# Split-operand attention scores, a query norm folded into the exponential, and weights split earlier in a one-core decoder layer

## The chip, the cores and the metric

The kernel runs on one core of a Trainium2 chip. The metric is device time of one execution in microseconds (us). The kernel before took 1689.93 us, the median of three runs (1689.31 to 1690.85).

## The reference

One layer of a hybrid decoder is computed for 1024 prompt tokens and 32 sample tokens (8 requests of 4), 1056 columns in all, with D = 1024: RMS norm, retention and gated linear recurrence with a common input projection, output projection and residual; then cross-attention into 256 memory tokens, and a SwiGLU feed-forward. The change touches the cross-attention (4 heads of 256 channels):

```python
m = _rmsnorm(mem, g_mem); k = (m @ w_xk); v = (m @ w_xv)            # memory keys and values, also outputs
q = (_rmsnorm(x, g_xa) @ w_xq).reshape(b, t, XA_HEADS, XA_HD)
s = einsum('bthd,bmhd->bhtm', q, mk) * (XA_HD ** -0.5)
p = softmax(s, axis=-1); o = einsum('bhtm,bmhd->bthd', p, mv)
x = x + o.reshape(b, t, -1) @ w_xo
```

Prompt tokens attend to the memory keys made here; each sample request has its own keys and values, read from a cache.

## The kernel before, in words

Activations lie with channels on the 128 partitions and tokens along the free dimension: eight tiles of 128 x 1056. Most products are made of split operands: a float32 number is written as a high part `h` (rounded to float32r by a ScalarE copy) and a low part `l` (the difference, by VectorE or GpSimd), and `mms` (line 226) does three single passes per product: hh, hl and lh. Some small products, the prompt scores among them, are plain float32 matmuls; the trace shows two records for each of these.

An `Item` is one block of 128 output channels: its weights come from DRAM in two halves of 256 KB (`wraw`, four buffers, by SyncE's queue), are split into `wh` (ScalarE) and `wl` (GpSimd, VectorE or one half each, by the item's `l_eng`), and are multiplied with all columns in groups of 384, 384 and 288. `run` goes through the items in order; the weights of the next item are split after the first piece of the present item (`w_split`), and those of a later one are loaded after its second group. The schedule is written by hand: each engine executes its instructions in the order in which the program issues them. Side work is written as generators; `tick()`, called after each piece of an item, advances every generator to its next `yield`. So "two yields" means two pieces later. An item in `c_items` has six pieces; the query items have twelve; an item with steps (`k_outer`) goes over k outermost, with a tick after each k.

The stages that matter, in order of time:

- `k_items` and `v_items` (about 520 to 580 us): memory keys and values, 256 columns. The key tile `k32` is kept in float32, and stored to the output `mk_o` from there.
- `c_items` (about 580 to 673 us): output projection with residual (line 993). ScalarE squares the sum (`sg`), GpSimd adds it to `acc` (line 340). The weights' low halves are made by GpSimd alone. Beside it runs `split_ahead`: it splits weights that are needed much later (17 blocks: ten halves of `w_xo`, seven of sums of `w_gate`) and stores both halves to DRAM (`pre_d`): load `praw`, `pwh` on ScalarE, `pwl` on GpSimd, two yields, two stores, then `PACE` = 3 more yields; two buffers each for `pwh` and `pwl`. After four items, the sample keys (`keyT`) and values (`vb`) are loaded too.
- `xq_items` (about 673 to 833 us): query projection; its first item is a `k_outer` whose steps split the normed-to-be input (`xh` on ScalarE, `xl` on VectorE, line 320). `rstd_bcast` (line 344) sums `acc` over channels on TensorE, takes the power -1/2 on GpSimd (line 327), broadcasts the factors of all columns to 128 partitions on TensorE (line 331), and copies them to `rbc`; the evacuation of every query item multiplies by it (line 1021).
- `attend(h)` runs as side work during the later query items and the first items after them: `stage_a` (scores, line 1194, row maximum, exponential), `stage_n` (division), `stage_b` (transposes of the probabilities and their split), `stage_c` (product with the split values). Each step of its list is two ticks apart. `sample_attend` does the same for the sample tokens, with the float32 queries.
- `ea_items`, `eb_items` (from about 833 us): product with `w_xo`; the second part reads the halves from `pre_d`.

Of the kernel before, what the change touches and what calls it, by code (L numbers as in the profile page):

```python
# [18 lines left out]
P = 128  # L19
# [28 lines left out]
LEAD = 3  # L48
LEADW = 3
KEYS = 4  # L50
PACE = 3
QUADS = ((0, 1), (0, 0), (1, 1), (1, 0))
DVE_L = 672
W1 = 4
# [41 lines left out]
def build(tc, ctx, a, outs):  # L96
# [4 lines left out]
    def newpool(name, bufs=1, stack=ctx, **kw):  # L101
        return stack.enter_context(tc.tile_pool(name=name, bufs=bufs, **kw))
# [17 lines left out]
    def sm():  # L120
        return psum("sm", 3)
# [7 lines left out]
    def tmp(nm):  # L129
        return gz.tile([P, GW], F32, name=nm, tag=nm)  # L130
# [4 lines left out]
    def btile(i, shape=None, dt=F32):  # L135
        return bp.tile(shape or [P, T], dt, name=f"b{i}", tag=f"b{i}")
# [20 lines left out]
    def side(gen):  # L157
        sides.append(gen)
        return gen
# [112 lines left out]
    def run(items):  # L272

        for it in items:
            i = done[0]
            assert wq[i] is it
            if it.start:
                it.start()
            w = splits.pop(i)
            if it.steps:  # L280
                k_outer(it, w)
            else:
                for n_, g in enumerate(it.order or range(len(it.cols))):
                    group(it, w, g, n_ == 0)
                    if n_ == 1:
                        w_raw()
            if it.steps or len(it.cols) < 2:
                w_raw()
            done[0] += 1
            if it.end:  # L290
                it.end()
# [630 lines left out]
    def mem_split():  # L922

        hh, ll = [[xtile(w_, k) for w_ in "hl"] for k in (3, 2)]
        kvs["memh"], kvs["meml"] = ([x[:, :4 * NMEM].rearrange("p (k t) -> p k t", k=4) for x in xx] for xx in (hh, ll))
        pt = sm()
        for i in range(2):
            bcast_cols(pt[:, i * P:(i + 1) * P], kvs["mr"][:, i:i + 1], P)
        kvs["rbm"] = tp.tile([P, T], F32, name="rbc", tag="rbc", bufs=1)
        dve.tensor_copy(kvs["rbm"][:, :NMEM], pt[:, :NMEM])  # L930
        kvs["k32"] = [btile(i, [P, 4, NMEM]) for i in range(2)]
        kvs["vh"] = [btile(2, [P, D], F32R), btile(3, [P, D], F32R)]

    def mem_split_k(k):
# [2 lines left out]
        act.activation(h_, src, AF.Copy, scale=gain("g_mem", k))  # L937
        dve.scalar_tensor_tensor(l_, src, gain("g_mem", k), h_.bitcast(F32), op0=ALU.mult, op1=ALU.subtract)

    def k32(m):  # L940
        return kvs["k32"][m // 4][:, m % 4]

    def kv_proj_item(wname, m, is_k, l_eng):
        def ev(pt, g):
            if is_k:
                t32 = k32(m)
            else:
                t32 = tmp("sg")[:, :NMEM]
            dve.tensor_tensor(t32, pt, kvs["rbm"][:, :NMEM], op=ALU.mult)

            def rest():
                yield
                if is_k:
                    yield
                    sp.dma_start(mk_o[m], t32)
                    return
                tt = sm()[:, :NMEM]
                for i in range(2):
                    pe.transpose(tt[:, i * P:(i + 1) * P], t32[:, i * P:(i + 1) * P], ident)
                st = tmp("z")[:, :NMEM]  # L960
                act.activation(st, tt, AF.Copy)
                ms = slice(m * P, (m + 1) * P)
                for i in range(2):
                    act.activation(kvs["vh"][i][:, ms], tt[:, i * P:(i + 1) * P], AF.Copy)
                    dve.tensor_tensor(kvs["vl"][i][:, ms], tt[:, i * P:(i + 1) * P], kvs["vh"][i][:, ms].bitcast(F32), op=ALU.subtract)
                yield
                sp.dma_start(mv_o[0, 0].rearrange("(i p) h d -> p i (h d)", p=P)[:, :, ms], st.rearrange("p (i e) -> p i e", i=2))

            side(rest())

        def start():
            if m == 0 and is_k:
                mem_split()
            if m == 0 and not is_k:
                kvs["vl"] = [btile(4, [P, D], F32R), btile(5, [P, D], F32R)]

        def mem_xs():
            return ([kvs[w_][k // 4][:, k % 4] for k in range(KT)] for w_ in ("memh", "meml"))

        it = Item(a[wname][m], KT, mem_xs, ev, cols=(slice(0, NMEM),), l_eng=l_eng, start=start)  # L980
        if is_k and m == 0:
            it.stepwise(range(KT), [lambda k=k: mem_split_k(k) for k in range(KT)])
        return it
# [27 lines left out]
                for b, order in enumerate(EB) for m in order]  # L1011
    for it in eb_items:
        it.l_eng, it.wide = "dve", True
    q32 = {}

    def xq_item(m):
        def start():
            q32[m] = act_tile(m)

        def ev(pt, g):  # L1020
            dve.tensor_tensor(q32[m][:, GS[g]], pt, rb["t"][:, GS[g]], op=ALU.mult)

        return Item(a["w_xq"][m], KT, xs, ev, start=start)

# [75 lines left out]
    def split_ahead():  # L1100
        jobs = [a["w_xo"][m][:, ks.start + (KH if m < XA else 0):ks.stop + (KH if m < XA else 0)]
                for m in range(KT) for ks in halves(KH if m < XA else KT)]

        def load(src):
            t = kv.tile([P, KH, P], F32, name="praw", tag="praw", bufs=4)
            sp.dma_start(t, src)
            return t

        def split(n, src):
            h_, l_ = (kv.tile([P, KH, P], F32R, name=nm, tag=nm, bufs=2) for nm in ("pwh", "pwl"))  # L1110
            split2(h_, l_, src, pool)
            yield
            yield
            for i, t in enumerate((h_, l_)):
                sp.dma_start(pre_d[n, i], t.bitcast(F32))
            for _ in range(PACE):
                yield

        raw = [load(j) for j in jobs[:2]]
        yield  # L1120
        yield
        for n in range(len(jobs)):
            yield from split(n, raw.pop(0))
            if n + 2 < len(jobs):
                raw.append(load(jobs[n + 2]))
        a21, a11, a22, a12 = [load(a["w_gate"][c][:, r * KH:(r + 1) * KH]) for r, c in QUADS]
        yield
        yield
        sm_ = kv.tile([P, KH, P], F32, name="psm", bufs=1)
        n0 = len(jobs)  # L1130
        at = {no: n0 + PRODUCTS.index(no) for no in PRODUCTS}
        pool.tensor_tensor(sm_, a21, a22, op=ALU.add)
        yield from split(at[5], sm_)
        pool.tensor_tensor(a21, a11, a21, op=ALU.subtract)
        yield from split(at[7], a21)
        yield from split(at[1], a11)
        pool.tensor_tensor(sm_, sm_, a11, op=ALU.subtract)
        yield from split(at[6], sm_)
        yield from split(at[4], a22)
        yield from split(at[2], a12)  # L1140
        pool.tensor_tensor(sm_, a12, sm_, op=ALU.subtract)
        yield from split(at[3], sm_)
# [17 lines left out]
        split_cols((new_x["h"][k], new_x["l"][k]), src, slice(0, T), scale)  # L1160

    xq_items[0].stepwise(ORD, [lambda k=k: split_next(k, st_c["x"][k], gain("g_xa", k)) for k in ORD], c_items[-1])
    side(split_ahead())
    run(c_items[:KEYS])
    load_values(0, 0)
    side(sample_keys())
    run(c_items[KEYS:])

    def exp_rows(pt, n, rows=P, tag="e", bufs=2):
        nm = tp.tile([P, 2], F32, name="nm", bufs=3)
        dve.tensor_reduce(nm[:rows, :n], pt, axis=AX.X, op=ALU.max, negate=True)
        e = kv.tile([P, n, NMEM], F32, name="e", tag=tag, bufs=bufs)
        s_ = tp.tile([P, 2], F32, name="sme", bufs=3)
        for i in range(n):
            act.activation(e[:rows, i], pt[:, i], AF.Exp, bias=nm[:rows, i:i + 1], accum_out=s_[:rows, i:i + 1])
        return e, s_

    def div_rows(e, s_, n, rows=P):  # L1180
# [5 lines left out]
    def attend(h):  # L1186
        es, phl = {}, {}

        def stage_a(it):
            pt = sm()  # L1190
            for tt in range(2):
                ts = slice(it * 256 + tt * P, it * 256 + (tt + 1) * P)
                for e_ in range(2):
                    pe.matmul(pt[:, tt * NMEM:(tt + 1) * NMEM], q32[2 * h + e_][:, ts], k32(2 * h + e_), start=(e_ == 0), stop=(e_ == 1))  # L1194
            es[it] = exp_rows(pt.rearrange("p (t m) -> p t m", t=2), 2)

        def stage_n(it):
            div_rows(*es[it], 2)
# [20 lines left out]
            for e_ in range(2):  # L1219
                act.activation(q32[2 * h + e_][:, it * 256:(it + 1) * 256], po[:, e_ * 256:(e_ + 1) * 256], AF.Copy)  # L1220

        for ops in ("a0", "n0a1", "b0", "n1a2", "c0", "b1", "n2a3", "c1", "b2", "n3c2", "b3", "c3"):
            for n_ in range(0, len(ops), 2):
                {"a": stage_a, "n": stage_n, "b": stage_b, "c": stage_c}[ops[n_]](int(ops[n_ + 1]))
            yield
            yield

# [77 lines left out]
        while min(finished.values()) <= h:  # L1305
            tick()

    def rstd_later(st, extra):
        yield
        yield from rstd_bcast(st["acc"], extra)  # L1310

    X.update(new_x)
    side(rstd_later(st_c, 1.0 / 16.0))
    new_o = {w_: [None] * KT for w_ in "hl"}

    def split_attended(k):
# [694 lines left out]
```

## Time and profile before

| | before |
|---|---|
| median of three runs | 1689.93 us |
| profiled execution | 1686.46 us, its span 1684.7 |
| TensorE busy | 1643.5 us (98%) |
| TensorE weight loads | 1581.3 us (94%) |
| VectorE, ScalarE, GpSimd busy | 834.5, 535.4, 612.7 us |
| granted TensorE clock, mean | 0.998 |

Times in rows are from the start of the span. A row of a timeline merges neighbouring instructions of one kind (x8 is eight of them); the bracket tells how long the engine was idle before it and what ended that. The durations of matmuls overlap, since they are pipelined: what one costs is read from start to start.

### The profile page before, as it was taken

To read this page: it belongs to the slowest core of one execution; us is meant where nothing else is said; L and a number is where in the kernel's file an instruction comes from. 1 tells how busy PE (TensorE), PEld (TensorE's weight loads), DVE (VectorE), ACT (ScalarE), POOL (GpSimd) and SP (SyncE) were. 2 spreads that over 40 slices of the span, in tenths; PEclk is the share of its full clock that TensorE was granted. 3 is DMA by queue.
4 is the path that set the end of the run, shared out by engine and by line. 5 is a ranking of instruction groups with operands and counts; after the bars stand their busy time and mean duration, and the time that the engine had idled before them with its cause. 6 is when DMAs were issued, how large, how long until landed. Compare 5 with 4: busy or idle time off the path is not lost.

```text
span 1684.7 us, 32950 instructions
## 1 busy us (share of the span) xinstructions
PE 1643.5 (98%) x13486; PEld 1581.3 (94%) x13486; DVE 834.5 (50%) x1576; ACT 535.4 (32%) x1078; POOL 612.7 (36%) x521
## 2 busy tenths in 40 slices
PE   7999999999999999999999999999999999999997
PEld 7999899999998899899899999999999999999987
DVE  6456566532236512433336766565666666322335
ACT  5222221332324523443433432323223234221221
POOL 2223133443434565410122255555555553222220
PEclk9999999999999999999999999999999999999999
DMA  8211111222214767353334522222222214222112
GB/s 279 68 51 44 61 54 39 71 83 65 64 55 144 239 218 254 120 168 114 122 108 157 160 80 77 83 77 76 77 77 85 81 64 154 93 88 93 53 55 104
DMA packets 111287, 175.00 MB, mean 104 GB/s; under 512 B 10592, under 2 KB 48768, under 8 KB 111136
## 3 DMA queue, kind: packets, MB, share of 16 engines
q1 hardware_dynamic: 109984, 171.75, 30.6%
q8 instruction: 106, 1.74, 0.4%
q10 hardware_dynamic: 1152, 1.14, 0.2%
q14 instruction: 45, 0.37, 0.1%
HBM read 137.66 MB, written 35.19 MB: 103 GB/s over the span
## 4 chain that ended last, share of the span: by engine, by line
PE 84%; issue 5%; DVE 5%; ACT 2%; POOL 2%; DMA 1%; POOLq 0%; DVEq 0%; ACTq 0%; SPq 0%
PE mm L232 53%; PE o L232 13%; PE sm L232 8%; PE sm L1194 1%; PE u L232 1%; PE sm L542 1%; PE sm L414 1%; PE o L446 1%; POOL wl L207 1%; PE u L433 1%; PE o L448 1%; DMA wraw<-in_w_xv_dram 1%; ACT wh L206 0%; PE sm L1238 0%; PE sm L467 0%
## 5 line engine op out<-in xcount | busy, mean ns | idle before, releaser
L232 PE MATMUL mm<-xh,wh 128*128 128x384 f32 (+3 forms) x1732 | 552.7, 326 | 8.8 <-ACT xh L787 6.2
L232 PE MATMUL mm<-xl,wh 128*128 128x384 f32 (+3 forms) x1732 | 536.1, 317 | 1.5 <-DVE xl L320 0.9
L232 PE MATMUL mm<-xh,wl 128*128 128x384 f32 (+3 forms) x1668 | 528.9, 317 | 6.3 <-DMA wl<-pre_d 3.2
L207 POOL TENSOR_TENSOR wl<-wraw,wh 128x512 fp32r<-128x512 f32 (+2 forms) x154 | 191.3, 1256 | 490.8 <-ACT wh L206 372.7
L232 PEld LDWEIGHTS mm<-xh,wh 128*128 128x128 f32 x1732 | 323.1, 189 | 23.2 <-issue 10.7
L232 PEld LDWEIGHTS mm<-xl,wh 128*128 128x128 f32 x1732 | 323.2, 189 | 4.4 <-DVE xl L320 1.4
L232 PEld LDWEIGHTS mm<-xh,wl 128*128 128x128 f32 x1668 | 314.9, 189 | 7.8 <-POOL wl L207 3.9
L206 ACT ACTIVATE wh<-wraw 128x512 fp32r<-128x512 f32 (+2 forms) x249 | 144.4, 600 | 301.5 <-PE mm L232 113.6
L232 PE MATMUL o<-xl,wh 128*128 128x264 f32 (+1 forms) x468 | 135.3, 289 | 0.2
L232 PE MATMUL o<-xh,wh 128*128 128x264 f32 (+1 forms) x468 | 135.1, 289 | 0.0
L232 PE MATMUL o<-xh,wl 128*128 128x264 f32 (+1 forms) x468 | 134.9, 288 | 0.0
L232 PE MATMUL mm<-n,wh 128*128 128x264 f32 (+2 forms) x586 | 123.2, 302 | 2.6 <-ACT n L206 1.6
L207 DVE TENSOR_TENSOR wl<-wraw,wh 128x512 fp32r<-128x512 f32 (+1 forms) x95 | 99.0, 1044 | 37.1 <-ACT wh L206 34.5
L1629 POOL TENSOR_TENSOR sil<-sil,rbc 128x528 f32<-128x528 f32 x44 | 63.2, 1460 | 142.1 <-ACT sil L1628 142.1
L1792 DVE TENSOR_TENSOR a<-mm,a 128x384 f32<-128x384 f32 (+1 forms) x71 | 37.3, 526 | 128.4 <-PE mm L232 128.3
L232 PEld LDWEIGHTS mm<-n,wh 128*128 128x128 f32 x586 | 95.3, 188 | 3.2 <-ACT n L206 1.9
L206 ACT ACTIVATE wh<-sum 128x512 fp32r<-128x512 f32 x84 | 52.9, 630 | 114.7 <-PE o L232 68.7
L232 PEld LDWEIGHTS o<-xl,wh 128*128 128x128 f32 x468 | 88.2, 188 | 0.9 <-POOL xl L317 0.8
L232 PEld LDWEIGHTS o<-xh,wh 128*128 128x128 f32 x468 | 88.2, 188 | 0.0
L232 PE MATMUL mm<-n,wl 128*128 128x264 f32 (+2 forms) x293 | 88.1, 301 | 0.0
L232 PEld LDWEIGHTS o<-xh,wl 128*128 128x128 f32 x468 | 87.9, 188 | 0.0
L1640 POOL TENSOR_TENSOR sil<-pt,sil 128x264 f32<-128x264 f32 x60 | 53.0, 904 | 56.9 <-DVE pt L1636 56.9
(403 smaller groups left out, 3016.3 us busy)
## 6 DMA issues: line engine op xcount, KB each, us to landing
wraw<-in_w_in_dram SPq DMA_DIRECT2D x62, 256.0 KB, 2.9
wraw<-in_w_up_dram SPq DMA_DIRECT2D x44, 256.0 KB, 3.2
p_d<-sil SPq DMA_DIRECT2D x40, 264.0 KB, 3.6
wraw<-in_w_gate_dram SPq DMA_DIRECT2D x40, 256.0 KB, 2.6
vb<-in_cache_mem_v_dram SPq DMA_DIRECT2D x32, 256.0 KB, 3.9
keyT<-in_cache_mem_k_dram SPq DMA_DIRECT2D x32, 256.0 KB, 4.7
wraw<-in_w_down_dram SPq DMA_DIRECT2D x32, 256.0 KB, 2.7
wh<-pre_d SPq DMA_DIRECT2D x22, 256.0 KB, 3.2
```

Source lines behind the costliest of these rows:

```text
L206: act.activation(h_, src, AF.Copy)
L207: e.tensor_tensor(l_, src, h_.bitcast(F32), op=ALU.subtract)
L232: pe.matmul(out, l_, r_, start=(first and i == 0), stop=(last and i == n - 1), **kw)
L414: pe.transpose(pt[:, c * P:(c + 1) * P], src[:, lo:lo + P], ident)
L433: pe.matmul(u[:, c * P:(c + 1) * P], ktok[:, cc * P:(cc + 1) * P], vtok[:, cc * P:(cc + 1) * P], start=True, stop=True)
L446: pe.matmul(dst, att[:, cc * P:(cc + 1) * P], vtok[:, cc * P:(cc + 1) * P], start=True, stop=(cc == 0))
L448: pe.matmul(dst, q[:, cc * P:(cc + 1) * P], S[:, cc - 1], start=False, stop=True)
L542: pe.matmul(pt[32 * j:32 * j + 32, c * w:(c + 1) * w], kk[:, lo:lo + 32], t_, start=True, stop=True)
L1194: pe.matmul(pt[:, tt * NMEM:(tt + 1) * NMEM], q32[2 * h + e_][:, ts], k32(2 * h + e_), start=(e_ == 0), stop=(e_ == 1))
L1629: pool.tensor_tensor(both, both, r[:, c2_], op=ALU.mult)
L1640: pool.tensor_tensor(dst, t, dst, op=ALU.mult)
L1792: dve.tensor_tensor(x2[m][:, GS[g]], pt, x2[m][:, GS[g]], op=ALU.add)
```

## The change

The keys are split as they are made (`kh`, `kl`), and the float32 copy is a temporary from which the output is stored. The queries are evacuated without the norm's factor; for the prompt columns the factor of each token (a column of `qn["p"]`, by partition) goes into the row maximum and into the exponential's scale, and only the sample columns are multiplied. `query_norm` therefore broadcasts the 32 sample columns alone. A new `stage_s` splits 256 query columns of a head ahead of `stage_a`, which does three passes per product. `split_ahead` runs at `PACE` 0 in a pool of its own (`spl`) with one buffer each for `pwh` and `pwl`; it is drained, and its pool closed, before the attention, and the queries' halves (`qp`) take the room.

```diff
-PACE = 3
+PACE = 0
...
-        kvs["k32"] = [btile(i, [P, 4, NMEM]) for i in range(2)]
+        kvs["kh"], kvs["kl"] = ([btile(i + j, [P, 4, NMEM], F32R) for i in range(2)] for j in (0, 6))
...
     def kv_proj_item(wname, m, is_k, l_eng):
         def ev(pt, g):
-            if is_k:
-                t32 = k32(m)
-            else:
-                t32 = tmp("sg")[:, :NMEM]
+            t32 = tmp("sg")[:, :NMEM]
             dve.tensor_tensor(t32, pt, kvs["rbm"][:, :NMEM], op=ALU.mult)
             def rest():
                 yield
                 if is_k:
-                    yield
+                    split2(*key(m), t32, dve)
                     sp.dma_start(mk_o[m], t32)
...
         def ev(pt, g):
-            dve.tensor_tensor(q32[m][:, GS[g]], pt, rb["t"][:, GS[g]], op=ALU.mult)
+            c = slice(GS[g].start, min(TP, GS[g].stop))
+            w = c.stop - c.start
+            dve.tensor_copy(q32[m][:, c], pt[:, :w])
+            if c.stop == TP:
+                dve.tensor_tensor(q32[m][:, TP:T], pt[:, w:w + TS], qn["s"], op=ALU.mult)
...
         def load(src):
-            t = kv.tile([P, KH, P], F32, name="praw", tag="praw", bufs=4)
+            t = spl.tile([P, KH, P], F32, name="praw", tag="praw", bufs=4)
...
-            h_, l_ = (kv.tile([P, KH, P], F32R, name=nm, tag=nm, bufs=2) for nm in ("pwh", "pwl"))
+            h_, l_ = (spl.tile([P, KH, P], F32R, name=nm, tag=nm, bufs=1) for nm in ("pwh", "pwl"))
...
-    side(split_ahead())
+    spl_ctx = ExitStack()
+    spl = newpool("spl", stack=spl_ctx)
+    ahead = side(split_ahead())
     run(c_items[:KEYS])
     load_values(0, 0)
     side(sample_keys())
     run(c_items[KEYS:])
+    drain(ahead)
+    spl_ctx.close()
+    qhl = {}
+    qp = [newpool("qp", stack=kv_ctx, reuse_waits="tile")]
...
+        dve.tensor_tensor(nm[:rows, :n], nm[:rows, :n], r, op=ALU.mult)
...
-            act.activation(e[:rows, i], pt[:, i], AF.Exp, bias=nm[:rows, i:i + 1], accum_out=s_[:rows, i:i + 1])
+            act.activation(e[:rows, i], pt[:, i], AF.Exp, bias=nm[:rows, i:i + 1], scale=r[:rows, i:i + 1], accum_out=s_[:rows, i:i + 1])
...
+        def stage_s(it, h=h):
+            ts = slice(it * 256, it * 256 + 256)
+            qhl[h, it] = [qp[0].tile([P, 2, 256], F32R, name=nm, tag=nm, bufs=2) for nm in ("qh", "ql")]
+            for e_ in range(2):
+                act.activation(qhl[h, it][0][:, e_], q32[2 * h + e_][:, ts], AF.Copy)
+                dve.tensor_tensor(qhl[h, it][1][:, e_], q32[2 * h + e_][:, ts], qhl[h, it][0][:, e_].bitcast(F32), op=ALU.subtract)
+
         def stage_a(it):
+            qh, ql = qhl.pop((h, it))
             pt = sm()
             for tt in range(2):
-                ts = slice(it * 256 + tt * P, it * 256 + (tt + 1) * P)
-                for e_ in range(2):
-                    pe.matmul(pt[:, tt * NMEM:(tt + 1) * NMEM], q32[2 * h + e_][:, ts], k32(2 * h + e_), start=(e_ == 0), stop=(e_ == 1))
-            es[it] = exp_rows(pt.rearrange("p (t m) -> p t m", t=2), 2)
+                tt_ = slice(tt * P, (tt + 1) * P)
+                mms(pt[:, tt * NMEM:(tt + 1) * NMEM], [((qh[:, e_, tt_], ql[:, e_, tt_]), key(2 * h + e_)) for e_ in range(2)])
+            es[it] = exp_rows(pt.rearrange("p (t m) -> p t m", t=2), 2, qn["p"][:, 2 * it:2 * it + 2])
...
-        for ops in ("a0", "n0a1", "b0", "n1a2", "c0", "b1", "n2a3", "c1", "b2", "n3c2", "b3", "c3"):
+        if (h, 0) not in qhl:
+            stage_s(0)
+            yield
+            yield
+        for ops in ("s1a0", "n0a1", "s2b0", "n1a2", "s3c0", "b1", "n2a3", "c1", "b2", "n3c2", "b3", "c3"):
+            if ops == "b3" and ready[0] > h + 1:
+                stage_s(0, h + 1)
...
-    def rstd_later(st, extra):
-        yield
-        yield from rstd_bcast(st["acc"], extra)
+    def query_norm(extra):
+        yield
+        st = sm()
+        for i in range(9):
+            rows = P if i < 8 else TS
+            pe.matmul(st[:rows, i:i + 1], st_c["acc"][:, i * P:i * P + rows], ones[:, 0:1], start=True, stop=True)
+        r = tp.tile([P, 16], F32, name="rr", tag="rr", bufs=2)
+        rstd_small(r[:, 0:8], st[:, 0:8], 8)
+        rstd_small(r[:TS, 8:9], st[:TS, 8:9], 1)
+        qn["p"] = tp.tile([P, 8], F32, name="qn", bufs=1)
+        dve.tensor_scalar(qn["p"], r[:, 0:8], extra, None, op0=ALU.mult)
+        yield
+        yield
+        yield
+        pt = sm()
+        bcast_cols(pt[:, :TS], r[:TS, 8:9], TS)
+        qn["s"] = tp.tile([P, TS], F32, name="qs", bufs=1)
+        dve.tensor_scalar(qn["s"], pt[:, :TS], extra, None, op0=ALU.mult)
...
-    side(rstd_later(st_c, 1.0 / 16.0))
+    side(query_norm(1.0 / 16.0))
```

## Rows read from the trace of the kernel before

**Rows 1.** The page: busy time by engine, and the chain that ended last.
```profile
PE 1643.5 (98%) x13486; PEld 1581.3 (94%) x13486; DVE 834.5 (50%) x1576; ACT 535.4 (32%) x1078; POOL 612.7 (36%) x521
...
PE 84%; issue 5%; DVE 5%; ACT 2%; POOL 2%; DMA 1%; POOLq 0%; DVEq 0%; ACTq 0%; SPq 0%
```
**Rows 2.** Busy us by stretch: PE, PEld, DVE, ACT, POOL; clock, DMA share, GB/s.
```profile
540.00:560.00 20.00, 18.66 (x172) 16.64 (x171) 14.32 (x29) 9.37 (x16) 10.38 (x9) 1.00 0.83 275
...
580.00:600.00 20.00, 20.00 (x122) 20.00 (x121) 5.26 (x8) 8.45 (x16) 13.01 (x10) 1.00 0.76 252
...
640.00:660.00 20.00, 20.00 (x126) 20.00 (x125) 2.69 (x5) 4.82 (x10) 11.93 (x12) 1.00 0.68 242
...
740.00:760.00 20.00, 20.00 (x148) 18.27 (x147) 7.16 (x13) 8.20 (x24) 1.28 (x1) 1.00 0.35 107
```
**Rows 3.** Timeline of PE around a score stage and a value stage: start, us, instruction.
```profile
704.48 0.34 PE L232 MATMUL mm<-xh,wl 128*128 128x384 f32 x1
704.65 1.89 PE L1194 MATMUL sm<-b,a 128*128 128x256 f32 x8
...
706.55 0.34 PE L232 MATMUL mm<-xl,wh 128*128 128x384 f32 x1
...
722.24 0.28 PE L232 MATMUL u<-ph,b 128*128 128x256 f32 x1
...
723.66 0.29 PE L232 MATMUL mm<-xh,wh 128*128 128x288 f32 x1
```
**Rows 4.** Two lines of the attention: duration in ns, min/median/max.
```profile
L1220 ACT ACTIVATE a<-u x32: 378/382/385, 723.9 to 885.6; 128x256 f32<-128x256 f32 x32
...
L1210 DVE TENSOR_TENSOR pl<-o,ph x16: 691/692/692, 716.1 to 882.7; 128x512 fp32r<-128x512 f32 x16
```
**Rows 5.** Timeline of PE in the first query item.
```profile
685.19 1.16 PE L331 MATMUL sm<-ident,rr 128*128 128x128 f32 x8 [1.33 <-POOL rr L327]
...
686.37 0.34 PE L232 MATMUL mm<-xl,wh 128*128 128x384 f32 x1
...
687.64 1.05 PE L331 MATMUL sm<-ident,rr 128*128 128x128 f32 x8
...
691.97 0.34 PE L232 MATMUL mm<-xh,wh 128*128 128x384 f32 x1
```
**Rows 6.** The same time on DVE and POOL; line 320 alone; line 327 by form.
```profile
677.88 4.39 DVE L320 SCALAR_TENSOR_TENSOR xl<-a,gains,xh 128x1056 fp32r<-128x1056 f32 x2 [1.64 <-ACT xh L319]
...
679.63 1.52 POOL L207 TENSOR_TENSOR pwl<-psm,pwh 128x512 fp32r<-128x512 f32 x1 [0.74 <-ACT pwh L206]
...
682.43 2.71 POOL L327 TENSOR_TENSOR rr<-rs,nhalf 128x8 f32<-128x8 f32 x1 [1.27 <-DVE rs L326]
...
L320 DVE SCALAR_TENSOR_TENSOR xl<-a,gains,xh x8: 1296/1308/2347, 672.1 to 684.8; 128x1056 fp32r<-128x1056 f32 x8
...
L327 POOL TENSOR_TENSOR rr<-rs,nhalf 128x8 f32<-128x8 f32 x2 | 4.4, 2180 | 5.0 <-DVE rs L326 5.0
```
**Rows 7.** Timeline of ACT late in the split-ahead work.
```profile
696.95 0.63 ACT L206 ACTIVATE pwh<-praw 128x512 fp32r<-128x512 f32 x1 [0.46 <-DMA pre_d<-pwh]
```
**Rows 8.** DMA issues from 608.5, 583 (to 648), 638.3: count, KB, us to landing.
```profile
pre_d<-pwl SPq DMA_DIRECT2D x1, 256.0 KB, 2.0
...
pre_d<-pwl SPq DMA_DIRECT2D x8, 256.0 KB, 3.4
...
pre_d<-pwl SPq DMA_DIRECT2D x1, 256.0 KB, 5.2
```
**Rows 9.** Timeline of SyncE's queue: stores of x behind items 1 and 2.
```profile
603.77 0.33 SPq L1080 DMA_DIRECT2D x_d<-a  x1
...
615.39 0.33 SPq L1080 DMA_DIRECT2D x_d<-a  x1
```
**Rows 10.** Timeline of POOL early in the output projection.
```profile
591.67 1.30 POOL L207 TENSOR_TENSOR pwl<-praw,pwh 128x512 fp32r<-128x512 f32 x1
593.31 2.53 POOL L207 TENSOR_TENSOR wl<-wraw,wh 128x512 fp32r<-128x512 f32 x2 [0.34 <-DMA praw<-in_w_xo_dram]
```

More of the change, by code (lines that the diff above doesn't have):

```diff
@@ L938, in mem_split_k, with key @@
         dve.scalar_tensor_tensor(l_, src, gain("g_mem", k), h_.bitcast(F32), op0=ALU.mult, op1=ALU.subtract)
-    def k32(m):
-        return kvs["k32"][m // 4][:, m % 4]
+    def key(m):
+        return tuple(kvs[w_][m // 4][:, m % 4] for w_ in ("kh", "kl"))
     def kv_proj_item(wname, m, is_k, l_eng):
         def ev(pt, g):
-            if is_k:
-                t32 = k32(m)
-            else:
-                t32 = tmp("sg")[:, :NMEM]
+            t32 = tmp("sg")[:, :NMEM]
             dve.tensor_tensor(t32, pt, kvs["rbm"][:, :NMEM], op=ALU.mult)
@@ L1013, in build @@
         it.l_eng, it.wide = "dve", True
-    q32 = {}
+    q32, qn = {}, {}
     def xq_item(m):
@@ L1128, in split_ahead @@
         yield
-        sm_ = kv.tile([P, KH, P], F32, name="psm", bufs=1)
+        sm_ = spl.tile([P, KH, P], F32, name="psm", bufs=1)
         n0 = len(jobs)
@@ L1167, in build, with exp_rows @@
     run(c_items[KEYS:])
-    def exp_rows(pt, n, rows=P, tag="e", bufs=2):
+    drain(ahead)
+    spl_ctx.close()
+    qhl = {}
+    qp = [newpool("qp", stack=kv_ctx, reuse_waits="tile")]
+    def exp_rows(pt, n, r, rows=P, tag="e", bufs=2):
         nm = tp.tile([P, 2], F32, name="nm", bufs=3)
         dve.tensor_reduce(nm[:rows, :n], pt, axis=AX.X, op=ALU.max, negate=True)
+        dve.tensor_tensor(nm[:rows, :n], nm[:rows, :n], r, op=ALU.mult)
         e = kv.tile([P, n, NMEM], F32, name="e", tag=tag, bufs=bufs)
@@ L1220, in stage_c @@
                 act.activation(q32[2 * h + e_][:, it * 256:(it + 1) * 256], po[:, e_ * 256:(e_ + 1) * 256], AF.Copy)
-        for ops in ("a0", "n0a1", "b0", "n1a2", "c0", "b1", "n2a3", "c1", "b2", "n3c2", "b3", "c3"):
+        if (h, 0) not in qhl:
[5 more added lines that the diff above has]
+                stage_s(0, h + 1)
             for n_ in range(0, len(ops), 2):
-                {"a": stage_a, "n": stage_n, "b": stage_b, "c": stage_c}[ops[n_]](int(ops[n_ + 1]))
+                {"s": stage_s, "a": stage_a, "n": stage_n, "b": stage_b, "c": stage_c}[ops[n_]](int(ops[n_ + 1]))
             yield
```

## The prediction

> **What bounds the kernel now.** I read the page first, then the busy time by stretch, then the instructions in order of time in the three places that the change touches. The page [rows 1] shows TensorE busy for 98% of the span and 84% of the chain that ended last, so a matmul pass taken away shortens the span, and anything that makes TensorE wait lengthens it. The stretches [rows 2] show where there is slack. In the output projection (`c_items`; 580 to 600 and 640 to 660 stand for its four stretches) TensorE is busy 20.00 of 20 us: nothing waits there now, and VectorE, ScalarE and GpSimd work 5.3, 8.5 and 13.0 us in the first 20. During the attention (740 to 760) it is just as full, with ScalarE and VectorE under half busy. From 540 to 560 (memory keys and values) it has 1.3 us of holes.
>
> The profiled execution took 1686.46 us (span 1684.7 and 1.8 around it), 3.5 below the median 1689.93 of the three timed runs. I work in differences and add them to the median.
>
> **Part 1, the scores.** One `stage_a` now is four float32 matmuls, eight records [rows 3]: they start at 704.65, and the second pass after them starts at 706.55, one 0.17 us pass after the first, so at 706.38: 1.73 us. Afterwards it is 2 x 2 x 3 = 12 passes of split operands with 256 columns. The trace has just that in `stage_c`: 12 passes from 722.24 to 723.66, 1.42 us. That is 0.31 us less; 4 heads x 4 stages x 0.31 = **-4.9 us**, on the engine that is the bound.
>
> What it costs elsewhere: each stage needs two ScalarE copies and two VectorE subtractions over 256 columns. A ScalarE copy of that size takes 0.38 us, and a VectorE subtraction of 512 columns 0.69 [rows 4], so some 0.4 for 256; 32 of each are 12 us per engine, spread over the 180 us in which each is under half busy [rows 2]. `stage_s` is issued two ticks ahead of its `stage_a`. A tick here is two k of three 0.17 us passes, 1.05 us, so the operands have 2.1 us for a chain of two copies and a subtraction, 1.2 us. TensorE waits only where ScalarE is over 0.9 us behind. The new two-column multiply lies in the score chain, not in TensorE's order. Between 0 (all hidden) and 16 x 0.3 = 5 us (each stage late by as much as it gained) I take **+1**.
>
> **Part 2, the query norm.** The eight 128-column broadcasts go. The first group of four, from 685.19, is over 0.17 before 686.37, so it took 1.0 us, and the second at 687.64 about as long [rows 5]; before the first TensorE waits 1.33 us for GpSimd's power. In their place VectorE waits for the power, since the `qn["p"]` multiply is issued right behind it, and behind that wait stand the splits of k = 5, 6 and 7, for which TensorE waits. What is late next is therefore VectorE's chain of splits, so I follow that. A split takes 1.31 us where GpSimd is idle, but the two at 677.88 took 2.12 and 2.27, 4.39 together [rows 6], beside GpSimd's `psm` sum and `pwl` split, which move away. So: the fourth and fifth splits end at 677.88 + 2 x 1.31 = 680.5, the small operations at 680.7, and the power follows. It took 2.71 here beside busy VectorE [rows 6]; the other one of 128x8 took 1.65 (mean of the two 2.18). With 1.65 it ends at 682.4, three splits at 686.4, and the last k (six passes of 0.17 us and three of 0.13, 1.45) at 687.9. Now the next item starts at 691.97 [rows 5]: **-4 us**; with the power at 2.71 it is -3. If the split-ahead work still ran beside it, the slow splits would stay and the wait would come on top: -1 to -2.
>
> **Part 3, keys split in place of kept.** Eight key items get one ScalarE copy and one VectorE subtraction more, 0.4 us each, in a stretch with holes [rows 2], where the chain runs weight load, split, free buffer, load. The key's store now reads a temporary with two buffers, which must land within two items (5.7 us); it is issued right after VectorE wrote it. From -0.5 to 8 x 0.4 = +3, I take **+1**.
>
> **Part 4, the weights split ahead, the step that decides.** `PACE` 3 to 0 takes the period of a split from five ticks to two, and `pwh`/`pwl` go from two buffers to one. All 17 splits then fall into the projection's 53 ticks (two ticks of loading, two per split, two more at the gate weights: the last is issued at tick 37, so `drain(ahead)` finds nothing). With one buffer, GpSimd's next `pwl` must wait until the store of the last one has landed. That such a wait is real, even with two buffers, is seen at 696.95, where ScalarE waits for a `pre_d` store [rows 7]. And GpSimd works in order: behind that `pwl` stand the `wl` halves of the projection's own weights, without which TensorE can't start an item.
>
> The period of the chain is 1.30 (`pwl`) + 0.1 + landing. Landing was 2.0 us with the queues empty, 3.4 in the median from 583 to 648, and 5.2 while keys and values are loaded [rows 8]. An item takes 11.62 us (stores of x at 603.77 and 615.39) [rows 9] and issues three splits, one per 3.87 us. I take 2.9 for the early landings, between the empty and the median one (the stretch gets denser), so 4.3 per split, and 4.5 (5.9 per split) beside the key loads.
>
> - Four splits after the first are issued in item 0, before the `wl` of item 2; now it is one. The split at 591.67 ends at 593.0 [rows 10], and nothing ahead of it changes. Three more periods end at 605.9, and the first `wl` half (2.53 for two) at 607.2. Item 2 has to start at 603.2, half a us before its predecessor's store. TensorE waits 4.0.
> - Item 3, behind three splits: 3 x 4.3 - 11.6 = 1.3. Item 4, behind two: none, 3.0 us in hand.
> - Item 5, behind three beside the key loads and a GpSimd sum: 17.7 + 1.3 - 11.6 - 3.0 = 4.4.
> - Item 6: 1.3, and part of a sum, 2.
>
> Together **+12 us** of TensorE waiting for `wl`, where there is none now. Lower bound, 2.0 for all landings: the first wait alone, 593.0 + 3 x 3.4 + 1.3 - 603.2 = 1.3. Upper, 3.4 and 5.2: 5.5 + 2.8 + 0 + 7.5 + 3 = 19.
>
> The Trainium skill, "DMA: Bandwidth & Descriptors", section "Rules for kernel authors", advises to issue a transfer early and wait for it late; a single buffer does the contrary. Its section "Anatomy of one DMA" gives 2.0 us plus bytes over 436 GB/s, from which 256 KB would take 2.6 us (an estimate); the trace has 2.0 alone and 3.4 in company. By 2.6 this part would come to +4 and the whole to a small gain.
>
> **Sum**: -4.9 + 1 - 4 + 1 + 12 = +5, so 1689.9 + 5 = **1695 us**.
>
> **Rivals.**
> A (forecast): GpSimd falls behind in the output projection; 1695, in its own range 1689 to 1702 (part 4 from 6 to 19). For it: the order of issue, and the landings of rows 8. Chance 0.52.
> B: the stores land nearly as if alone, because a chain that waits for itself keeps the queues empty. At landings of 2.0 to 2.7 (halfway to the median), periods of 3.4 to 4.1, part 4 costs 1.3 to about 5, and the sum is -5.6 to -2: 1684 to 1688, I take 1685. It decides below a period of about 4.1. For it: the 2.0 of an empty queue; against it: the 3.4 with half the split traffic. Chance 0.30.
> C: the scores gain nothing, because `stage_a` waits for `ql` on ScalarE and VectorE: +5 in place of +1, with some 3 us in part 4, so 1690. Against it: both engines are under half busy. Chance 0.12.
> D: the keys' extra splits and the store out of a temporary lengthen the chain of weight loads by its full 3 us and more, on top of A: 1698 or above. Chance 0.06.
>
> **How the numbers follow.** About 0.2% (3.4 us) is what can be told from no change, so the bounds are 1686.5 and 1693.3. A: slower 0.44, same 0.07, faster 0.01. B: faster 0.26, same 0.04. C: same 0.08, slower 0.02, faster 0.02. D: slower 0.04, same 0.02. Faster 0.29, same 0.21, slower 0.50. The ends of all unknown costs make 1682 (1690 - 4.9 + 0 - 4 - 0.5 + 1.3) to 1711 (1690 - 4.9 + 5 - 1 + 3 + 19); with a tenth left out at each end 1683 to 1704.
>
> **What would show it.** Scores: twelve passes of 256 columns, 1.42 us per stage. Norm: one 32-column broadcast is left, VectorE waits some 1.7 us for GpSimd's power, all splits take 1.3 us, and the first query item is 4 us shorter. Part 4: between the start of the output projection and the query norm, waits of TensorE for `wl` of about 12 us, the first and one of the longest at the start of item 2, and GpSimd's `pwl` released by stores of `pwl`. I am wrong if TensorE stays at 20.00 of 20 us through that projection (then B, faster), or if waits for `ql` appear in the attention (C).

## The result, and the profile after

The changed kernel takes 1698.68 us (median of 4 runs, 1697.31 to 1701.14), beside 1690.13 for the kernel before in the same session: a ratio of 1.0058 [1.0045, 1.0071] on record, slower by more than the 0.2% that can be told. (These two medians alone give 1.0051, or 8.6 us; 1.0058 of 1690 is 9.8 us. Sums below are no finer than that gap.) Forecast were 1695 us and, as the likeliest case, rival A. The profiled execution took 1697.31 us, span 1695.5.

The page of the changed kernel, as in [rows 1]:
```profile
PE 1644.1 (97%) x13534; PEld 1584.3 (93%) x13534; DVE 851.3 (50%) x1639; ACT 550.3 (32%) x1118; POOL 611.6 (36%) x521
...
PE 81%; DVE 5%; DMA 4%; issue 4%; ACT 2%; POOL 2%; SPq 1%; POOLq 0%; DVEq 0%; ACTq 0%
```
TensorE is busy as long as before, but its share of the chain falls by three points and the DMAs' share rises by three: something now waits for transfers. The stretches of the output projection, after, beside [rows 2] (columns the same):
```profile
600.00:620.00 20.00, 15.23 (x96) 14.44 (x94) 2.42 (x5) 5.39 (x11) 10.91 (x10) 1.00 0.79 267
620.00:640.00 20.00, 18.56 (x102) 18.24 (x103) 2.13 (x4) 5.30 (x11) 15.31 (x14) 0.91 0.66 226
640.00:660.00 20.00, 18.55 (x116) 17.99 (x114) 2.45 (x5) 5.07 (x10) 13.66 (x13) 1.00 0.81 278
660.00:680.00 20.00, 15.43 (x78) 14.92 (x79) 1.71 (x4) 5.83 (x12) 13.44 (x12) 0.83 0.65 237
680.00:700.00 20.00, 19.66 (x120) 19.27 (x119) 9.48 (x11) 11.34 (x15) 6.50 (x7) 0.93 0.22 82
```
From 600 to 680, where before 20.00 of 20 us were busy in three stretches and 19.65 in the fourth, 15.2 to 18.6 are. (In the last stretch stands the norm, which before had 18.11 there, so it can't be compared.) The granted clock (third column from the right) is under 1 in three stretches, where it was 1.00 throughout. The waits of TensorE from 585 to 690 (us in total, times, longest):
```profile
PE mm L232 <- ACT wh L206: 6.3, 3, 3.9
PE mm L232 <- POOL wl L207: 6.0, 4, 2.4
```
12.3 us, half of them for `wl`, half for `wh`. Two of them in the timeline of PE:
```profile
606.78 0.45 PE L232 MATMUL mm<-xh,wl 128*128 128x384 f32 x1 [2.37 <-POOL wl L207]
...
663.52 0.69 PE L232 MATMUL mm<-xh,wh 128*128 128x384 f32 x1 [3.88 <-ACT wh L206]
```
After the longest, a pass that has 0.34 us at the full clock [rows 3] has a record of 0.69. Not every wait is followed by slow passes: around the first (0.82 us for `wh` and 2.37 for `wl`) the clock stays at 1.00.
```profile
604.00:608.00 4.00, 1.63 (x9) 1.31 (x9) 0.00 (x0) 0.68 (x2) 3.75 (x4) 1.00 0.87 242
```
GpSimd at the start of the projection, as in [rows 10]:
```profile
591.91 1.29 POOL L207 TENSOR_TENSOR pwl<-praw,pwh 128x512 fp32r<-128x512 f32 x1
597.28 1.29 POOL L207 TENSOR_TENSOR pwl<-praw,pwh 128x512 fp32r<-128x512 f32 x1 [4.08 <-DMA pre_d<-pwl]
600.73 1.30 POOL L207 TENSOR_TENSOR pwl<-praw,pwh 128x512 fp32r<-128x512 f32 x1 [2.16 <-DMA pre_d<-pwl]
604.25 1.26 POOL L207 TENSOR_TENSOR pwl<-praw,pwh 128x512 fp32r<-128x512 f32 x1 [2.22 <-DMA pre_d<-pwl]
605.47 2.50 POOL L207 TENSOR_TENSOR wl<-wraw,wh 128x512 fp32r<-128x512 f32 x2
```
Each later `pwl` here waits for the store of the last one, and the `wl` halves of item 2 start at 605.47, behind the fourth. ScalarE does the same one step ahead, as the row of [rows 7] showed once, with 0.46 us:
```profile
595.54 0.63 ACT L206 ACTIVATE pwh<-praw 128x512 fp32r<-128x512 f32 x1 [7.13 <-DMA pre_d<-pwh]
...
610.59 0.63 ACT L206 ACTIVATE pwh<-praw 128x512 fp32r<-128x512 f32 x1 [5.91 <-DMA pre_d<-pwh]
```
Landings from 583 to 648 (count, KB, median us), as in [rows 8]:
```profile
pre_d<-pwh SPq DMA_DIRECT2D x13, 256.0 KB, 2.9
pre_d<-pwl SPq DMA_DIRECT2D x12, 256.0 KB, 2.1
```
A score stage after in the timeline of PE, as in [rows 3]:
```profile
724.27 0.40 PE L232 MATMUL sm<-b,qh 128*128 128x256 f32 x2
...
725.70 0.34 PE L232 MATMUL mm<-xh,wh 128*128 128x384 f32 x1
```
Twelve passes in 1.43 us, as worked out. The exponential takes 561 ns with a scale (mean of 32; 469 before), and the subtraction for `ql` 0.42 us in the median. No wait for `ql` is among TensorE's. The query norm on VectorE, as in [rows 6]:
```profile
698.13 0.21 DVE L326 TENSOR_SCALAR rs<-sm 128x8 f32<-128x8 f32 x2
700.06 0.17 DVE L1340 TENSOR_SCALAR qn<-rr 128x8 f32<-128x8 f32 x1 [1.71 <-POOL rr L327]
700.14 1.32 DVE L320 SCALAR_TENSOR_TENSOR xl<-a,gains,xh 128x1056 fp32r<-128x1056 f32 x1
701.37 2.34 DVE L320 SCALAR_TENSOR_TENSOR xl<-a,gains,xh 128x1056 fp32r<-128x1056 f32 x1
703.64 2.35 DVE L320 SCALAR_TENSOR_TENSOR xl<-a,gains,xh 128x1056 fp32r<-128x1056 f32 x1
...
706.69 0.56 DVE L1020 COPY a<-mm 128x384 f32<-128x384 f32 x1
```
And on GpSimd:
```profile
700.50 2.10 POOL L207 TENSOR_TENSOR wl<-wraw,wh 128x512 fp32r<-128x512 f32 x1
702.57 2.31 POOL L207 TENSOR_TENSOR wl<-wraw,wh 128x512 fp32r<-128x512 f32 x1
```
VectorE waits 1.71 us for the power, as forecast (1.7). Of its last three `xl` the first, begun before GpSimd's `wl`, takes 1.32 us as forecast, but the other two take 2.34 and 2.35 beside it: 5.84 for the three together.

### The profile page after: what moved, and what is told of

Read it like the earlier page. It is cut to its first block, busy times and chain, and to the rows that moved or that the text cites. A ratio compares the mean times of both kernels' runs of the same rounds, so it can differ in the third digit from the quotient of the medians.

```text
span 1695.5 us, 33149 instructions
## 1 busy us (share of the span) xinstructions
PE 1644.1 (97%) x13534; PEld 1584.3 (93%) x13534; DVE 851.3 (50%) x1639; ACT 550.3 (32%) x1118; POOL 611.6 (36%) x521
## 4 chain that ended last, share of the span: by engine, by line
PE 81%; DVE 5%; DMA 4%; issue 4%; ACT 2%; POOL 2%; SPq 1%; POOLq 0%; DVEq 0%; ACTq 0%
PE mm L232 51%; PE o L232 12%; PE sm L232 9%; PE u L232 1%; DMA a<-in_x_T_dram 1%; PE sm L542 1%; DMA pre_d<-pwh 1%; PE sm L414 1%; PE o L446 1%; DMA wraw<-in_w_xv_dram 1%; PE u L433 1%; PE o L448 1%; POOL wl L207 1%; POOL pwl L207 1%; DMA pre_d<-pwl 1%
## 5 line engine op out<-in xcount | busy, mean ns | idle before, releaser
L990 DVE TENSOR_TENSOR a<-mm,a 128x384 f32<-128x384 f32 (+2 forms) x55 | 27.2, 495 | 108.5 <-PE mm L232 105.8
```

Of the source, the lines that this page charges most:

```text
L990: dve.tensor_tensor(x[:, c], pt, x[:, c], op=ALU.add)
```

## The experiments

Ratios are to the kernel before, run on the same chip. The theory: one buffer each for `pwh` and `pwl`, at a split every two ticks, stops ScalarE and GpSimd on stores, and the projection's own `wh` and `wl` wait behind. Rivals: only one of the two chains; the traffic of the stores, whatever the buffers; the norm or scores.

**e1_pwl_two and e2_pwh_two: a second buffer for one of the two.**
```
-  ... name=nm, tag=nm, bufs=1) for nm in ("pwh", "pwl"))
+  ... name=nm, tag=nm, bufs=n_) for nm, n_ in (("pwh", 1), ("pwl", 2)))   # e2: 2 and 1
```


> The changed kernel with one edit: two buffers for pwl (one for pwh, as changed). Theory (GpSimd's next pwl waits for the store of the last one, and the projection's wl halves wait behind it): the wait for a pwl store goes; what is left is ScalarE's wait for the pwh store, 0.6 + 0.1 + 2 to 3 us, under the 3.87 us between splits. TensorE's waits in the output projection fall from 12.3 to 4 us or less, the granted clock there returns to 1.00, the time to 1684 to 1689. Rival (the denser DMA traffic itself delays weights and splits): the traffic is the same, so 1697 to 1700.

> The changed kernel with two buffers for pwh and one for pwl. Theory: GpSimd still waits for each pwl store, so most of the waits stay; ScalarE's own wait goes, so that the part of TensorE's wait put down to wh (6.3 us) moves to wl or shrinks: 8 to 12 us of waits in all, 1693 to 1699. Rival (the waits are ScalarE's, behind pwh): they go, 1684 to 1689. Rival (DMA traffic): no change.

Measured 1700.30 us, 1.0068 [1.0055, 1.0080], and 1699.49 us, 1.0063 [1.0051, 1.0075]: neither gains. TensorE's waits from 585 to 690 with two `pwl`, then with two `pwh`:
```profile
PE mm L232 <- ACT wh L206: 7.9, 2, 6.8
PE mm L232 <- POOL wl L207: 5.3, 4, 1.4
```
```profile
PE mm L232 <- POOL wl L207: 12.1, 4, 4.6
PE mm L232 <- ACT wh L206: 1.0, 1, 1.0
```
The sum stays at 13 us and goes over to the engine whose buffer is single. The forecast's chain through GpSimd is real, but it is one of two: freed alone it gives nothing.

**e3_pace_one: one tick more between splits, buffers as changed.**
```
-PACE = 0
+PACE = 1
```


> The changed kernel with PACE 1: a split every three ticks (5.8 us) in place of two, single buffers as changed. Theory: the period of the store chain, 4 to 4.5 us, is shorter than 5.8, so TensorE waits 2 us at most in the output projection, beside the first splits, which follow k steps of 1.45 us; the last two splits fall beside the first query item and cost 1 to 2 us there: 1683 to 1688. Rival (DMA traffic): the same bytes in a stretch half as long again, about half of the loss stays, 1692 to 1696.

Measured 1684.40 us, 0.9974 [0.9963, 0.9985]. The projection:
```profile
600.00:620.00 20.00, 20.00 (x127) 20.00 (x126) 2.59 (x5) 7.22 (x15) 17.11 (x16) 1.00 0.86 292
```
TensorE is full again at the full clock, and 14 us come back (1.0058 less 0.9974), more than the 12.3 of waits. The stores are as many; their distance alone has changed.

**e4_wl_vector: the projection's `wl` by VectorE, out of GpSimd's order.**
```
+    for it in c_items:
+        it.l_eng = "dve"
```


> The changed kernel with the low halves of the projection's weights made by VectorE in place of GpSimd (VectorE is busy 2.4 of 20 us there). Theory: TensorE's wait for wl (6.0 us) goes, since wl no longer stands behind pwl; the wait for wh (6.3 us) stays in part, since ScalarE still takes pwh in order, and pwh waits for pwl: 4 to 7 us of waits, 1689 to 1694. Rival (DMA traffic): no change.

Measured 1707.53 us, 1.0117 [1.0101, 1.0133], the other way. The waits from 585 to 690:
```profile
PE mm L232 <- DVE a L990: 15.6, 4, 6.5
```
VectorE now stands in order at `wl`, which needs ScalarE's late `wh` (39.4 us of such waits from 575 to 700), and TensorE waits for the evictions behind it. Moving an operation to an idle engine moved the wait, and made it longer.

**e5_both_two and e6_both_two_pace_one: two buffers of both (`psm` put elsewhere), at `PACE` 0 and 1.**
```
-  ... bufs=1) for nm in ("pwh", "pwl"))
+  ... bufs=2) for nm in ("pwh", "pwl"))
-  sm_ = spl.tile([P, KH, P], F32, name="psm", bufs=1)
+  sm_ = kv.tile([P, KH, P], F32, name="psm", tag="pT", bufs=1)
```


> The changed kernel, PACE 0, with two buffers for pwh and for pwl; psm takes the room of pT, which is free then. After one kind alone had gained nothing: theory that either chain alone (ScalarE behind the pwh store, GpSimd behind the pwl store) is enough to hold the output projection: with both freed TensorE's waits there fall from 12.3 to 4 us or less, 1681 to 1687. Rival (the landings are late because the queues are crowded, whatever the number of buffers, and the loads and stores of the projection with them): 8 us or more of waits stay, 1693 to 1700.

> As the kernel with two buffers of each, and PACE 1. Theory: no wait is left in the output projection that the kernel with PACE 1 and single buffers did not have; what it gains on that one is the slack of ScalarE at the start of the query projection: 1681 to 1685. Rival: nothing hangs on the buffers at this pace: 1683 to 1686.

Measured 1685.38 us, 0.9981 [0.9972, 0.9990], and 1685.43 us, 0.9979 [0.9970, 0.9988]. At `PACE` 0 TensorE's waits from 585 to 690 are 3.4 us for `wl`, and none for `wh`:
```profile
PE mm L232 <- POOL wl L207: 3.4, 4, 1.4
```
while the stores land later than in the changed kernel (583 to 648, count, KB, us):
```profile
pre_d<-pwh SPq DMA_DIRECT2D x14, 256.0 KB, 4.9
pre_d<-pwl SPq DMA_DIRECT2D x14, 256.0 KB, 3.8
```
So the stores' traffic is not the cause; the single buffers are, both together, at a split every two ticks. At `PACE` 1 the second buffers give nothing (e3 1684.40, e6 1685.43), as that run's rival had it. The 3.4 us of waits in e5 are followed by no slow pass: its clock from 600 to 680 is 1.00.

**e7_scores_undone and e8_norm_undone: the kernel of e6 with one other part taken back.** In e7 keys and scores are float32 again (`k32`, four matmuls in `stage_a`, no `stage_s`); in e8 the norm is that of before (`rstd_bcast`, the product with `rb["t"]` in `xq_item`, no scale in `exp_rows`).

> The kernel with two buffers of each and PACE 1, with the scores as before (float32 passes, keys kept in float32, no stage_s); the norm's factors stay in the exponential's scale. Theory: the split scores are worth 4.9 less 0 to 2 for the key splits and waits, so this one is 3 to 5 us slower than its parent. Rival (what the scores gain is lost to waits for ql): within 1 us of the parent, and waits for ql in the parent.

> The kernel with two buffers of each and PACE 1, with the query norm as before (all columns broadcast, evacuation by a multiply). Theory: the norm's edit is worth about 2 us as the trace of the changed kernel has it (18.5 us less 16.5 from the end of the output projection to the first evacuation of a query item), so this one is 1 to 4 us slower than its parent. Rival (VectorE's wait for the power eats what the broadcasts cost): within 1 us.

Measured 1691.22 us, 1.0018 [1.0009, 1.0026], and 1682.28 us, 0.9969 [0.9956, 0.9981]. Scores and keys are worth 5.8 us (1691.22 less 1685.43). e8's median is 3.2 us under that of e6, but the two intervals overlap, and the forecast that it would be 1 to 4 us slower is not borne out. The single runs differ in mean clock: those at 0.997 took 1682.21 and 1682.98 us in e6 and 1682.16, 1682.28 and 1684.28 in e8, and only two of e6's eleven runs had that clock, but three of e8's five. So at `PACE` 1 no worth of the norm's edit, of either sign, is shown.

**e9_norm_folded: e6 with the factor folded into the power.**
```
-  rstd_small(r[:, 0:8], st[:, 0:8], 8)
-  rstd_small(r[:TS, 8:9], st[:TS, 8:9], 1)
-  qn["p"] = tp.tile([P, 8], ...); dve.tensor_scalar(qn["p"], r[:, 0:8], extra, None, op0=ALU.mult)
+  qn["p"] = tp.tile([P, 16], F32, name="qn", bufs=1)
+  sc = 1.0 / D / extra ** 2, EPS / extra ** 2
+  rstd_small(qn["p"][:, 0:8], st[:, 0:8], 8, *sc)
+  rstd_small(r[:TS, 8:9], st[:TS, 8:9], 1, *sc)
```


> As e6_both_two_pace_one, but the factor of 1/16 is folded into the scale and the addend of the power, which GpSimd then writes straight into `qn`: VectorE no longer waits for the power before the three `xl` of its queue. If that wait, which lets GpSimd's `wl` start beside the `xl`, is what the query norm's edit costs: the first query item's eviction 1 to 2 us sooner than in e6_both_two_pace_one, and 1682 to 1684 us (ratio to the kernel before 0.996 to 0.997). If the cost is in the exponentials with a scale and the copies in the evictions: no change, 1685 us (0.998). By the prediction's own figure of 4 us for this part it would be 1678 to 1679 us once the wait is gone (0.9935).

Measured 1685.01 us, 0.9978 [0.9968, 0.9988]: no change, and the first eviction does not come sooner: 10.5 us after `rs` (682.91 to 693.43), where e6 has 8.6 and e8 9.0. VectorE's wait has gone and its splits are quick, but TensorE waits in its place. VectorE in e9:
```profile
683.05 3.76 DVE L320 SCALAR_TENSOR_TENSOR xl<-a,gains,xh 128x1056 fp32r<-128x1056 f32 x3
```
TensorE's longest wait from 676 to 702, and its stretches at 684 and 688:
```profile
PE sm L331 <- POOL rr L327: 3.1, 1, 3.1
```
```profile
684.00:688.00 4.00, 0.93 (x7) 0.70 (x5) 3.40 (x4) 2.20 (x4) 4.00 (x3) 0.98 0.00 0
688.00:692.00 4.00, 4.00 (x16) 3.94 (x17) 0.19 (x1) 0.00 (x0) 2.29 (x2) 0.59 0.28 88
```
The one broadcast left needs the second, smaller power, and TensorE, which works in order, stands at it for 3.1 us (1.1 in e8, where the large broadcasts need only the first). After that hole the clock is 0.59. Since e9 is 2 us later than e6 at this eviction and no slower in all, the way from `rs` to the eviction alone does not tell what the edit is worth. By what was expected, no change would mean that the cost lies in the exponentials and copies; since one wait took the other's place, the run does not decide that.

**e10_norm_alone and e11_split_alone: one part of the change alone on the kernel before.** e10 has the norm's edit with the exponentials' scale; e11 the lines of the `spl` pool, `PACE` 0 and one buffer each.

> The kernel before with the query norm's edit alone. The prediction's price is -4 us (ratio 0.9976; with the -1 to -2 us for the case of work beside it, 0.999). If e8_norm_undone told its sign rightly, it is 0 to +3 us (1.000 to 1.002).

> The kernel before with the split-ahead in front of the attention, one buffer each of `pwh` and `pwl`, and nothing else of the change. If TensorE's waits for `wl` and `wh` are all that it costs: +12 us (ratio 1.007). If the clock that falls after them comes on top as the trace after the change shows it, +12 and +7, 19 us (1.011). From the differences of the runs so far (1.0058 less 0.9974): +14 us (1.0084). If the scores and norm of the change had a part in the waits, it is under +8 us (1.005).

The norm alone: 1694.01 us, 1.0031 [1.0018, 1.0043], slower by 5.7 us by the medians and 5.2 by the ratio, above the 0 to +3 expected. VectorE in its profile:
```profile
685.03 0.21 DVE L326 TENSOR_SCALAR rs<-sm 128x8 f32<-128x8 f32 x2
686.94 2.95 DVE L1324 TENSOR_SCALAR qn<-rr 128x8 f32<-128x8 f32 x1 [1.70 <-POOL rr L327]
689.80 5.80 DVE L320 SCALAR_TENSOR_TENSOR xl<-a,gains,xh 128x1056 fp32r<-128x1056 f32 x3
...
697.36 0.56 DVE L1023 COPY a<-mm 128x384 f32<-128x384 f32 x1 [1.05 <-PE mm L232]
```
GpSimd beside it:
```profile
687.39 1.25 POOL L207 TENSOR_TENSOR wl<-wraw,wh 128x512 fp32r<-128x512 f32 x1
688.61 1.25 POOL L1138 TENSOR_TENSOR praw<-praw 128x512 f32<-128x512 f32 x1
```
And the stretches from 688 to 696:
```profile
688.00:692.00 4.00, 1.07 (x4) 0.84 (x4) 4.00 (x3) 1.15 (x2) 3.26 (x3) 0.78 0.16 62
692.00:696.00 4.00, 4.00 (x15) 4.00 (x14) 4.00 (x3) 0.00 (x0) 2.49 (x2) 0.50 0.37 134
```
From `rs` to the first query item's eviction it takes 12.3 us, before 9.1 (682.19 to 691.25): the multiply for `qn`, 0.17 us elsewhere, lasts 2.95, until GpSimd's `wl` and sum have ended (689.86), and the splits behind it take 1.30, 2.32 and 2.33 beside GpSimd's `pwl` and `wl`. TensorE is busy 1.07 of 4 us, then runs at 0.50. That is 3.3 of the 5.7 us. This profile is of the slowest of its six runs (1700.4 us) and reaches `rs` 2.8 us later than the kernel before (685.03 for 682.19), ahead of anything that the edit touches, so the rest is left open.

The split alone: 1705.51 us, 1.0098 [1.0084, 1.0112], 17.2 us over before. Its waits from 585 to 700:
```profile
PE mm L232 <- POOL wl L207: 8.0, 4, 2.9
PE mm L232 <- ACT wh L206: 2.4, 3, 1.1
```
And two stretches:
```profile
600.00:620.00 20.00, 16.74 (x95) 16.18 (x94) 2.13 (x4) 5.49 (x11) 10.59 (x10) 0.91 0.76 250
...
640.00:660.00 20.00, 16.84 (x86) 16.27 (x85) 1.57 (x3) 5.08 (x10) 13.63 (x13) 0.83 0.78 262
```
Waits of 10.4 us, and 0.09, 0.17 and (680 to 700) 0.07 of 20 us of clock, 6.6 together: 17.0. The 6.6 are an upper bound, since TensorE waited in a part of that time.

**e12_after_norm_undone: the changed kernel with the norm of before.**

> The kernel after the change with the query norm's edit alone undone (the norm of before; scores and split-ahead as changed). After this change TensorE arrives late at the norm, has rows of full busy time through it (692 to 716 us) and waits for none of its steps; so if the norm's edit costs only by what TensorE waits for there, it costs nothing here, and gains the eight broadcasts that it takes away: 1699 to 1701 us, ratio 1.0063 to 1.0075 (from the single runs, 16.5 for the split ahead, -5.8 for the scores and 9.8 in all leave -0.9 for the norm). If the edit costs by its exponentials and copies, or wherever it stands, as in e10_norm_alone: 1693 to 1696 us, ratio 1.003 to 1.0045. By the prediction's -4 us: 1702 to 1703 us, 1.008.

Measured 1700.24 us, 1.0067 [1.0053, 1.0081], by the ratios 1.5 us over the changed kernel: on the side of a gain by the edit, but the intervals don't part the two. VectorE in its profile:
```profile
698.93 0.21 DVE L326 TENSOR_SCALAR rs<-sm 128x8 f32<-128x8 f32 x2
...
708.93 0.56 DVE L1018 TENSOR_TENSOR a<-mm,rbc 128x384 f32<-128x384 f32 x1 [0.53 <-PE mm L232]
```
From `rs` to the first eviction 10.0 us, with the edit 8.6 (698.13 to 706.69): 1.4 gained on this way. In both TensorE comes late and slowed to this place, and waits 0.3 us at most for either form's steps.

## Why the prediction came out as it did

The measured time lies in the range, on the side forecast and in rival A's own range, but three parts of the sum were off and partly made up for each other.

**Parts 1 and 3, right, and a little short.** 1.43 us a stage against 1.42, no wait for `ql`. I charged +1 for waits and +1 for the keys (part 3); with the keys it is worth 5.8 us, not 2.9. The keys' own +1 does not show: the last pass of item 1 of the output projection, behind them, starts at 602.69, before the change at 602.95. Rivals C and D fall.

**Part 2, the size is wrong.** -4 was taken from "a split takes 1.31 us where GpSimd is idle" and from GpSimd being idle once the split-ahead had gone. The two splits ahead of `rs` do take 1.3 (2.55 together, at 695.67); but the query items' own `wl`, which before came after the power and behind the splits, now run while VectorE has been held back by its wait, and cost two of the three `xl` 1.0 us each: the price for GpSimd's company, which I had from the trace [rows 6], belonged to these too. In this kernel the edit gives 1.4 us on the way to the first eviction; of the whole time e12 shows no more than that it lies on the same side (1.5, not parted from nothing). My price for work beside it, -1 to -2, had the wrong sign: e10 shows +5.7 by the medians. What I left out there is that the eight broadcasts were also TensorE's work while it waited. One pair of runs shows it: with the same quick splits, TensorE is busy 0.93 us of 684 to 688 without them (e9) and 2.89 with them (e8), and only e9's clock falls behind it. But e6, which lacks them too, is busy for 2.91 us there and keeps its clock; so that the same holds in e10 is argued, not shown.

**Part 4, the mechanism and the waits are right, the clock is missing.** Forecast were 12 us of TensorE waiting, the fourth `pwl` done at 605.9 and item 2 as the first to starve; measured 12.3, 605.5, and item 2 is the first. That the sizes agree so well is partly luck. The periods of `pwl` were 5.4, 3.5 and 3.5 us (its starts above), not three of 4.3, and the split among the items was not as I had it: 3.2 at item 2 (0.82 for `wh` and 2.37 for `wl`) for 4.0, 3.0 at item 3 for 1.3, 1.1 at item 5 for 4.4, and 4.9 at item 6 (with the longest, 3.88, at 663.5) for 2. Half of the waits is ScalarE's: I followed `pwl` alone, although the row that I cited for the wait [rows 7] was ScalarE's. e1 and e2 show that the two chains stand in for each other, e5 that both buffers have to be freed. The term that failed is the slow clock, which I put at nothing. In the changed kernel's stretches of 4 us the clock is under 1 at 620 to 628, 660 to 672 and 696 to 704; what it lacks of full, times 4 us, makes 6.9 us, an upper bound, since TensorE waited in a part of that time; from start to start of the passes it is about 5.5 (1.6, 2.1, 1.7). The first two follow the waits at items 3 and 6. The third follows none of them: just before it stand the norm's sums, matmuls of one column (694.09 to 696.26), which the kernel before has as well, at 1.00. e11 and e12 show the same fall there (0.93 from 680 to 700; 0.69 from 696 to 700), e3 and e5 do not; what brings it on is open. The two worst stretches:
```profile
660.00:664.00 4.00, 0.48 (x1) 0.48 (x2) 0.14 (x1) 1.68 (x4) 0.97 (x1) 0.90 1.03 401
664.00:668.00 4.00, 2.95 (x10) 2.44 (x10) 0.00 (x0) 0.40 (x1) 4.00 (x5) 0.50 0.70 251
```
TensorE was nearly idle in the first, and runs at half the clock, 1.2 GHz, in the second. The Trainium skill, "TensorE: Matmul & The Clock Gate", Part 1, says that the slow state is the default and activity lifts it, and puts the ramp's cost under 1% of a typical kernel's span. Here it is 0.4% at most, so the trace agrees; yet that is nearly half of what the waits cost.

**Sum.** -5.8 (e7), -1.5 (e12) and +17.2 (e11) make +9.9, beside 9.8 by the ratio. That it closes to 0.1 is luck: the three were taken in three different kernels, two by medians and one by ratios, and each is known to 2 or 3 us. By ratios alone they are -6.6, -1.5 and +16.5, 8.4 in all. Forecast were +5: 5.2 too little for part 4, 2.5 too much gain for part 2, 2.9 too little gain for parts 1 and 3. Rival B (landings as if alone) had the landings nearly right, `pwl` 2.1 and `pwh` 2.9 in the median, yet the waits came: two of the three periods (3.5) are under its point of decision, 4.1, but that was for one chain, and the other engine stood as well. The Trainium skill's fit from which the prediction estimated 2.6 us ("Anatomy of one DMA") is for transfers that GpSimd issues; these stores go by SyncE's queue. The Trainium skill's rule that the prediction weighed, "DMA: Bandwidth & Descriptors", "Rules for kernel authors", issue early and wait late, is what e3 and e5 bear out: a later wait for the store gives 14 and 13 us.

**Open.** Why the runs of e6 and e9 had the higher mean clock less often than those of e8. In the profiles of e6 and e8 (0.994 and 0.997) the clock is 1.00 at the norm in both (676 to 700) and differs far behind it: 0.96 against 1.00 from 1400 to 1440, and 0.89 against 0.97 from 960 to 980. No run parts the norm's edit from that.

## What to carry to other kernels

Where two engines work in pairs on single buffers that a store must empty, follow both in order, and ask which other work stands behind each; here a tick of distance (e3) or a second buffer of both (e5) gave 14 and 13 us back, a second buffer of one nothing. A hole in a full TensorE can cost more than its own length: in e11 10.4 us of waits cost 17. But it need not: after the holes of item 2, and after those of e5, the clock stayed at 1.00, so look at the granted clock behind each. Matmuls that look superfluous may be what TensorE does while it waits; before taking them away, see what it would stand at instead.

## What the runs showed of the hardware

VectorE and GpSimd hold each other up when both work on such tiles. In the changed kernel's rows at 700 they look like taking turns: an `xl` that starts alone takes 1.32 us, the next two 2.34 and 2.35, and the two `wl` between them 2.10 and 2.31, where 1.25 is usual (2.50 for two at 605.47). Beside GpSimd's power `xl` keeps its 1.3 us (e9: 3.76 for three), and the power grows: in e8 two take 4.68 us, in the changed kernel, with VectorE waiting, 2.15. The Trainium skill, "SBUF — State Buffer", "SBUF: two separate sides", says that the two share a pair of ports which one instruction holds whole while the other stands still. The trace agrees, nearly: three `xl` (3.76) and two `wl` (2.5) one after the other would take 6.3 us (an estimate from the rows), and their union here is 5.84; and the `qn` of e10 ends with GpSimd's second sum.

The `pwl` stores land in 2.1 us in the median, and still ScalarE stood for up to 7.1 us on a `pwh` store in the same queue. The median hides what stands ahead: that `pwh` was ready at 588.43, its store was issued at 589.90, behind two loads of `x` of 528 KB each, and landed 5.5 us later. The wait of 5.91 us is of the same kind: ready at 603.23, issued at 604.40 behind two weight loads and a store of `x`, landed after 6.1.
